# An order of its own for the first group of layer 1: four tiles' projections and turns ahead of the fifth tile's

## The chip, the cores and the metric

The kernel runs on one core of one Trainium2 chip. The metric is the device time of one execution in microseconds. A core has a matrix engine (TensorE, PE in the profile), a vector engine (VectorE, DVE), a scalar engine (ScalarE, ACT), GpSimd (POOL) and a queue engine (SyncE, SP) that here issues DMAs. "PEld" is the loading of weights into the matrix engine.

## The reference, cut to what matters

Two trunk layers work on 512 latent tokens and 256 context tokens of width 1024. Layer 0 is differential attention, layer 1 is 2-D neighbourhood attention; each is followed by a squared-ReLU MLP. The change lies in layer 1, whose mixer is, for 16 heads of 64:

```python
q_l = heads_q(h_lat, w_q, NA_HEADS, q_gain)        # project, then RMS norm per head
k_l, v_l = heads_kv(h_lat, w_kv, NA_HEADS, k_gain)
k_c, v_c = heads_kv(h_ctx, w_kv, NA_HEADS, k_gain)
...
s_all = concat(q @ k_band + bias (a window of the grid), q @ k_c)
o = softmax(s_all) @ (v_band, v_c)
y_l = o @ w_o
```

The result of layer 1 is asked for latent tokens alone, so the two context tiles need keys and values and no queries.

## The kernel before

**Tiles and products.** The 768 tokens are six tiles of 128: tiles 0 and 1 are context, tiles 2 to 5 latent. "The fifth tile" is tile 4. Each product is made of three matmuls on split operands: an operand is kept as a rounded part and a remainder, and `PASSES` runs three of the four combinations. Splitting a weight tile is `wsplit`: a copy on ACT (L146) and a subtraction (L152), which in layer 1 DVE makes.

**Layer 1's attention** works in eight groups of two heads (`group1`). A group's steps, each called by a word of an order:

- `Q0a` to `Q5b` (`project`): the projection of one token tile, in two halves of 12 matmuls (L414), 256 columns wide for tiles 0 and 1 and 384 for the others, into a bank "PA" of which there are three (`PS_ATTN1`, A=3). Behind the second half comes `qk_normed`: ACT copies the queries and keys out of the bank (L421), squares them (L425); DVE sums (L427); POOL takes the power -0.5 (L302); DVE scales (L429). The values are split beside it, by ACT (L626) and DVE (L627, the last reader of the bank).
- `U0`, `U2`, `U4` (`turn`): the normed queries and keys of two tiles are transposed by PE into a bank PA (L640 queries, L642 keys), scaled and split by ACT and DVE (L442, L443 for queries; L450 to L454 for keys) with copies on POOL (L456). `U0` also issues the load of the group's bias on SP (L635).
- `S`, `T`, `V`: scores, transposed weights, weighing.
- `w0` to `w3`: SP loads a raw weight tile of the next group (L130, two buffers R). `c0` to `c3`: that tile is split. They are not steps of the group itself.

**Order.** `run` goes through the words of an order and calls the step of group c, c-1 (one prime) or c-2 (two). Words of groups that do not exist are skipped. The instructions of PE, SP and POOL keep this order (`PINNED`), and so do the splits among each other (`pinned=True`); the other instructions of ACT and DVE are placed by a scheduler when the kernel is built, so an order does not fix their sequence. On the chip each engine goes through the sequence that it was given.

For the first group (c = 0) no earlier group exists, so what is left of `CYCLE1` is

```
w0 w1 Q0a Q1a c0 w2 Q0b Q1b Q2a Q2b Q3a Q4a c1 w3 Q3b U0 Q4b c2 U2 Q5a Q5b c3
```

and the next group's order begins with `Q0a U4' Q1a`, so that the turn of tiles 4 and 5 of the first group comes behind `Q0a` of the second. The first group's own weights are loaded and split before the end of layer 0's MLP, into buffers H; the later groups' lie in buffers W. The first projections run between the last matmuls of that MLP (L986) and the transposes of its result (L334), whose modulated parts for layer 1 are made by ACT (L337) and DVE (L339, L340) two tiles at a time, tiles 4 and 5 last.

Of the kernel before, what the change touches and what calls it, by code (L numbers as in the profile page):

```python
# [26 lines left out]
GROUPS1 = 8  # L27
# [18 lines left out]
X6 P4b V5' P5a P5b O4' O5'"""  # L46
CYCLE1 = """w0 w1 Q0a T3'' U4' Q1a c0 w2 V2'' V3'' Q0b S0' Q1b Q2a S1' Q2b Q3a T0' S2' Q4a c1 w3 T1' Q3b S3' V0' U0
Q4b c2 U2 Q5a T2' Q5b c3 V1'"""
LAST1 = """Q0a T3'' U4' Q1a c0 x0 x1 V2'' V3'' Q0b S0' Q1b X0 x2 Q2a S1' Q2b X1 Q3a T0' S2' Q4a T1' Q3b X2 S3' V0'
U0 Q4b U2 Q5a T2' Q5b V1'"""  # L50
END1 = """x3 x4 T3'' c1 U4' V2'' V3'' S0' X3 x5 P2a S1' c2 X4 P3a T0' S2' X5 T1' P4a B0 S3' V0' V1' P2b T2' x6 P3b
# [976 lines left out]
class Mods:  # L1028
# [5 lines left out]
    def load(self, early=False):  # L1034
        if self.todo:
            self.ready.append(self.b.mod_load(*self.todo.pop(0), early))
# [16 lines left out]
def run(order, c, steps, load, split, **others):  # L1053


    for word in order.split():
        kind, num, h = word[0], word[1:].rstrip("'"), c - word.count("'")
        if kind == "w":
            load(h + 1, int(num))
        elif kind == "c":  # L1060
            split(h + 1, int(num))
        elif kind in others:
            others[kind](num)
        elif h in steps:
            steps[h](kind, 2 * int(num[0]) + (num[1:] == "b") if kind == "Q" else int(num))


def hybrid_block(tc, a, out):
    nc = tc.nc
    with ExitStack() as ctx, ExitStack() as st:  # L1070
# [9 lines left out]
        with b.psum_phase("ps0", **PS_HEAD0):  # L1080
# [7 lines left out]
            heads = {0: b.head0(0, accs=accs)}  # L1088
        w = {1: b.load_qkv(a["wqa"], 1, "WB")}
        with b.psum_phase("psA", **PS_ATTN0):  # L1090
            proj, raws = {}, {}

            def load(h, k):
                if h < HEADS0:
                    raws[h, k] = b.wraw(a["wqa"][h, k], 768)

            def split(h, k):
                if h < HEADS0:
                    w.setdefault(h, []).append(b.wsplit(raws.pop((h, k)), 768, tag=("WA", "WB")[h % 2], pinned=True))
                elif k < 3:  # L1100
                    proj["weights"](k)

            with tc.manual_schedule(engines=PINNED):
                heads[1] = b.head0(1, w[1], hT)
                for c in range(2, HEADS0):
                    if c == HEADS0 - 1:
# [7 lines left out]
                own = {"P": lambda n: proj["step"](2 * int(n[0]) + (n[1] == "b")), "B": lambda _: proj["begin"](),  # L1114
                       "x": lambda n: proj["fetch"](int(n)),
                       "X": lambda n: proj["split"](int(n), (nc.gpsimd, nc.vector)[int(n) % 3 == 2])}
# [3 lines left out]
        with b.psum_phase("psB", **PS_MLP0):  # L1120
# [11 lines left out]
            w1 = []  # L1132
# [23 lines left out]
        with b.psum_phase("psC", **PS_ATTN1):  # L1156
            heads, done, proj, w, raws = {}, [], {}, {0: w1}, {}

            def load(g, k):
                if g < GROUPS1:  # L1160
                    raws[g, k] = b.wraw(a["wqb"][g, k], 768)

            def split(g, k):
                if g < GROUPS1:
                    w.setdefault(g, []).append(b.wsplit(raws.pop((g, k)), 768, eng=nc.vector, tag="W1", pinned=True))
                else:
                    proj["weights"](k)

            with tc.manual_schedule(engines=PINNED):
                own = {"P": lambda n: proj["step"](2 * int(n[0]) + (n[1] == "b")), "B": lambda _: proj["begin"](),  # L1170
                       "x": lambda n: proj["fetch"](int(n)),
                       "X": lambda n: proj["split"](int(n), nc.gpsimd)}
                for c in range(GROUPS1):
                    if c == GROUPS1 - 1:
                        b.close("W1")
                        b.open("right", W=1, ST=2)
                        proj.update(b.project(1, a["wob"], b.oT1, 2, lambda i: b.x2[i - 2], 'HQ', 'QH', 'S1', done))
                    heads[c] = b.group1(c, w.setdefault(c, []), hT1, split=proj.get("split_last"))
                    run(CYCLE1 if c < GROUPS1 - 1 else LAST1, c, heads, load, split, **own)
                b.close("W1")  # L1180
                b.open("left", W=3)
                run(END1, GROUPS1, heads, load, split, **own)
            proj["end"]()
            xh1, hT3 = done
# [82 lines left out]
```

## Time and profile before

| what | us |
|---|---|
| median of 3 runs (1872.67 to 1874.06) | 1873.72 |
| the profiled execution, its own time | 1877.93 |
| its span | 1876.1 |
| PE busy in the span | 1750.8 |
| DVE busy | 1265.9 |
| POOL busy | 1025.6 |
| ACT busy | 948.6 |

The rows of the trace come from the profiled execution and are counted from the start of its span; about 1.8 us of its time lie outside the span. Layer 1's first group of attention lies at about 1105 to 1154 us.

### The profile page before, as it was taken

To read this page: it belongs to the slowest core of one execution; us is meant where nothing else is said; L and a number is where in the kernel's file an instruction comes from. 1 tells how busy PE (TensorE), PEld (TensorE's weight loads), DVE (VectorE), ACT (ScalarE), POOL (GpSimd) and SP (SyncE) were. 2 spreads that over 40 slices of the span, in tenths; PEclk is the share of its full clock that TensorE was granted. 3 is DMA by queue.
4 is the path that set the end of the run, shared out by engine and by line. 5 is a ranking of instruction groups with operands and counts; after the bars stand their busy time and mean duration, and the time that the engine had idled before them with its cause. 6 is when DMAs were issued, how large, how long until landed. Compare 5 with 4: busy or idle time off the path is not lost.

```text
span 1876.1 us, 27723 instructions
## 1 busy us (share of the span) xinstructions
PE 1750.8 (93%) x10046; PEld 1530.5 (82%) x10046; DVE 1265.9 (67%) x2333; ACT 948.6 (51%) x2002; POOL 1025.6 (55%) x962
## 2 busy tenths in 40 slices
PE   6989999996999999999999998999998989999988
PEld 5868888984789888888887987988997777887766
DVE  4587777786665465465466776777777567777685
ACT  4476777765344333333333345777776354544432
POOL 3655666653335565555555633343345557788774
PEclk9999999997999999999999998999998989999989
DMA  8122222224536656646642321121212434334432
GB/s 332 43 85 79 88 87 70 68 84 149 175 115 167 180 163 169 186 163 173 181 162 86 118 96 59 61 87 66 65 61 90 141 103 133 124 124 149 142 116 77
DMA packets 88554, 225.97 MB, mean 120 GB/s; under 512 B 9248, under 2 KB 24544, under 8 KB 82272
## 3 DMA queue, kind: packets, MB, share of 16 engines
q1 hardware_dynamic: 78928, 211.19, 35.0%
q10 hardware_dynamic: 9488, 13.00, 1.9%
q8 instruction: 79, 1.29, 0.3%
q14 instruction: 59, 0.48, 0.1%
HBM read 205.91 MB, written 18.25 MB: 119 GB/s over the span
## 4 chain that ended last, share of the span: by engine, by line
PE 62%; DVE 11%; ACT 8%; POOL 8%; issue 6%; DMA 5%; ACTq 0%; POOLq 0%; DVEq 0%
PE PD L850 18%; PE PA L414 14%; POOL W L152 6%; PE PB L910 5%; PE PA L910 5%; PE PA L758 4%; DMA R<-in_w_dram 3%; PE PA L986 2%; PE PB L558 2%; PE PA L263 2%; ACT W L146 2%; PE PS L523 2%; PE PQ L404 1%; PE PS L662 1%; PE PB L707 1%
## 5 line engine op out<-in xcount | busy, mean ns | idle before, releaser
L152 POOL TENSOR_TENSOR W<-R,W 128x512 fp32r<-128x512 f32 x270 | 406.6, 1533 | 164.9 <-ACT W L146 162.8
L850 PE MATMUL PD<-Q,W 128*128 128x384 f32 (+2 forms) x1992 | 390.5, 346 | 12.5 <-DVE Q L340 5.9
L850 PEld LDWEIGHTS PD<-Q,W 128*128 128x128 f32 x1992 | 345.9, 189 | 43.8 <-issue 7.8
L146 ACT ACTIVATE W<-R 128x1024 fp32r<-128x1024 f32 (+1 forms) x165 | 168.2, 1023 | 201.0 <-PE PD L850 35.3
L152 POOL TENSOR_TENSOR W<-N,W 128x512 fp32r<-128x512 f32 x98 | 137.8, 1427 | 141.9 <-ACT W L146 141.6
L910 PE MATMUL PB<-W,H 128*128 128x512 f32 x738 | 191.9, 396 | 6.4 <-DVE Q L918 4.4
L910 PE MATMUL PA<-W,H 128*128 128x512 f32 x732 | 191.1, 397 | 5.1 <-DVE H L918 4.0
L414 PE MATMUL PA<-W,Q 128*128 128x384 f32 (+1 forms) x1008 | 176.3, 327 | 1.1 <-ACT H L452 1.1
L910 PEld LDWEIGHTS PB<-W,H 128*128 128x128 f32 x738 | 139.1, 190 | 38.9 <-DVE Q L918 5.3
L910 PEld LDWEIGHTS PA<-W,H 128*128 128x128 f32 x732 | 137.7, 190 | 38.1 <-DVE H L918 5.7
L302 POOL TENSOR_TENSOR SQ<-SQ,half 128x4 f32<-128x4 f32 (+1 forms) x96 | 94.0, 980 | 126.7 <-DVE SQ L427 125.6
L414 PEld LDWEIGHTS PA<-W,Q 128*128 128x128 f32 x1008 | 160.3, 193 | 1.3 <-ACT H L452 1.3
L146 ACT ACTIVATE W<-N 128x1024 fp32r<-128x1024 f32 x49 | 51.9, 1058 | 149.1 <-PE PA L910 66.4
L414 PE MATMUL PA<-WB,H 128*128 128x384 f32 x576 | 108.5, 340 | 0.8 <-DVE Q L475 0.8
L758 PE MATMUL PA<-W,H 128*128 128x512 f32 x384 | 96.9, 402 | 6.4 <-ACT H L749 4.4
L414 PEld LDWEIGHTS PA<-WB,H 128*128 128x128 f32 x576 | 98.7, 188 | 1.8 <-DVE Q L475 1.1
L850 PE MATMUL PD<-H,W 128*128 128x512 f32 (+1 forms) x408 | 94.7, 382 | 0.0
L868 DVE SCALAR_TENSOR_TENSOR H<-N,H 128x512 fp32r<-128x512 f32 (+1 forms) x57 | 66.3, 1167 | 39.8 <-ACT H L867 39.5
L758 PEld LDWEIGHTS PA<-W,H 128*128 128x128 f32 x384 | 71.6, 192 | 24.1 <-ACT H L749 4.8
L529 ACT ACTIVATE E<-PS,SA 128x768 f32<-128x768 f32 (+1 forms) x96 | 73.0, 760 | 35.3 <-DVE SA L528 32.0
L528 DVE TENSOR_REDUCE SA<-PS 128x1 f32<-128x768 f32 (+1 forms) x96 | 74.5, 776 | 21.0 <-ACT E L529 11.5
L850 PEld LDWEIGHTS PD<-H,W 128*128 128x128 f32 x408 | 75.0, 192 | 14.9
(258 smaller groups left out, 3563.4 us busy)
## 6 DMA issues: line engine op xcount, KB each, us to landing
R<-in_w_dram SPq DMA_DIRECT2D x121, 512.0 KB
M<-in_wmod_dram SPq DMA_DIRECT2D x48, 1024.0 KB
N<-in_w_dram SPq DMA_DIRECT2D x49, 512.0 KB
R<-in_wqa_dram SPq DMA_DIRECT2D x32, 384.0 KB
R<-in_wqb_dram SPq DMA_DIRECT2D x32, 384.0 KB
Y<-in_rpb_dram SPq DMA_DIRECT2D x48, 128.0 KB
bias<-Y SPq DMA_DIRECT2D x48, 128.0 KB
X<-bias SPq DMA_DIRECT2D x8, 768.0 KB
```

What stands on the lines that cost most here:

```text
L146: high = nc.scalar.activation(w[:, 0, :n], raw, AF.Copy)
L152: low = (eng or nc.gpsimd).tensor_sub(w[:, 1, o:e], raw[:, o:e], w[:, 0, o:e].bitcast(F32))
L263: nc.tensor.matmul(ps[32 * q:32 * q + 32, 0:256], self.silu[:, kt, :], raws[kt], start=kt < 4, stop=kt >= 4)
L302: nc.gpsimd.tensor_tensor(r, ss, self.half[:, :n], op=ALU.pow)
L414: nc.tensor.matmul(acc[:, :n], hT[kt][:, x, P * i:P * i + P], w[kt // 2][:, y, o:o + n], start=(kt == 0 and p == 0), stop=(kt == KT - 1 an ...
L523: nc.tensor.matmul(s[:, c0:c1], q[:, m, P * i:P * i + P], k[:, m, c0:c1], start=p == 0, stop=p == 1)
L528: nc.vector.tensor_reduce(mx, s, op=ALU.max, axis=AX, negate=True)
L529: nc.scalar.activation(e[:, m, :nk], s, AF.Exp, bias=mx[:, 0:1], accum_out=sm[:, m:m + 1])
L758: nc.tensor.matmul(ps, oHL[h][:, x, c:c + P], w[h // 2][:, y, 512 * (h % 2):512 * (h % 2) + 512], start=(first and h == hs[0] and p == 0), ...
L850: nc.tensor.matmul(ps[:, at:at + b1 - b0], w[kt // 4][:, x, o:o + P], hT[kt][:, y, b0:b1], start=(kt == 0 and p == 0), stop=(kt == KT - 1 ...
L868: nc.vector.scalar_tensor_tensor(u[:, 1], src, 1.0, u[:, 0].bitcast(F32), op0=ALU.mult, op1=ALU.subtract)
L910: nc.tensor.matmul(ps, u[:, x, f, P * i:P * i + P], w[:, y, 512 * f:512 * f + 512], start=(f == 0 and p == 0), stop=(f == 1 and p == 2))
```

## The change

The first group gets an order of its own, `START1`. It names each word once, so that nothing is added to or taken from the work; words without a step for c = 0 are not written.

```diff
+START1 = """w0 w1 Q0a Q1a c0 Q0b Q1b w2 Q2a Q2b Q3a U0 Q3b c1 w3 U2 Q4a Q4b c2 Q5a Q5b c3"""
 LAST1 = ...
@@
                     heads[c] = b.group1(c, w.setdefault(c, []), hT1, split=proj.get("split_last"))
-                    run(CYCLE1 if c < GROUPS1 - 1 else LAST1, c, heads, load, split, **own)
+                    run(START1 if c == 0 else CYCLE1 if c < GROUPS1 - 1 else LAST1, c, heads, load, split, **own)
```

Against what was left of `CYCLE1`: up to `Q3a` the matmuls stand as before. `U0` moves ahead of `Q3b`; `U2` moves ahead of `Q4a` and stands right behind `Q3b` (with `c1 w3` between, which are not PE's); `Q4a` moves behind `U2`, so that both halves of tiles 4 and 5 run in one piece. `c1` and `w3` move behind `Q3b`, `w2` behind `Q1b`, and with it the load of the bias in `U0` stands ahead of `w3` on SP.

## Rows read from the trace of the kernel before

**Rows 1.** The page: busy time of each engine.
```profile
PE 1750.8 (93%) x10046; PEld 1530.5 (82%) x10046; DVE 1265.9 (67%) x2333; ACT 948.6 (51%) x2002; POOL 1025.6 (55%) x962
```

**Rows 2.** Timeline of PE: start, duration, line, count [idle before, releaser].
```profile
1118.60 3.96 PE L414 MATMUL PA<-H,Q 128*128 128x256 f32 x26
...
1122.43 1.31 PE L414 MATMUL PA<-H,Q 128*128 128x384 f32 x6
...
1123.60 1.48 PE L414 MATMUL PA<-H,Q 128*128 128x384 f32 x7
...
1127.48 0.66 PE L334 MATMUL PB<-ident,N 128*128 128x128 f32 x4 [0.26 <-ACT Y L337]
1131.78 9.13 PE L414 MATMUL PA<-H,Q 128*128 128x384 f32 x36 [3.64 <-DVE H L627]
1140.75 0.38 PE L642 MATMUL PA<-ident,Y 128*128 128x128 f32 x2
1140.88 2.36 PE L414 MATMUL PA<-H,Q 128*128 128x384 f32 x12
1143.08 0.27 PE L640 MATMUL PA<-ident,Y 128*128 128x128 f32 x1
...
1144.13 0.33 PE L640 MATMUL PA<-ident,Y 128*128 128x128 f32 x1 [0.68 <-DVE Y L429]
...
1144.46 4.49 PE L414 MATMUL PA<-H,Q 128*128 128x384 f32 x24
1148.79 1.59 PE L414 MATMUL PA<-W,Q 128*128 128x256 f32 x12
...
1153.80 0.33 PE L640 MATMUL PA<-ident,Y 128*128 128x128 f32 x1 [3.20 <-DVE Y L429]
...
1153.99 4.61 PE L414 MATMUL PA<-W,Q 128*128 128x256 f32 x24
```

**Rows 3.** Timeline of ACT, same columns.
```profile
1125.50 3.76 ACT L337 ACTIVATE Y<-PB,mB,mA 128x256 f32<-128x256 f32 x8 [4.45 <-PE PB L334]
...
1129.87 0.28 ACT L421 ACTIVATE Y<-PA 128x128 f32<-128x128 f32 x1
...
1130.92 0.90 ACT L146 ACTIVATE W<-R 128x768 fp32r<-128x768 f32 x1
...
1149.21 0.39 ACT L421 ACTIVATE Y<-PA 128x256 f32<-128x256 f32 x1
...
1149.79 0.85 ACT L146 ACTIVATE W<-R 128x768 fp32r<-128x768 f32 x1
```

**Rows 4.** Timeline of DVE, same columns.
```profile
1131.44 0.68 DVE L627 TENSOR_TENSOR H<-PA,H 128x128 fp32r<-128x128 f32 x3
...
1134.68 0.29 DVE L429 SCALAR_TENSOR_TENSOR Y<-Y,SQ 128x128 f32<-128x128 f32 x1
...
1150.67 0.96 DVE L152 TENSOR_TENSOR W<-R,W 128x768 fp32r<-128x768 f32 x1 [0.58 <-ACT W L146]
```

**Rows 5.** PE in slices of 2 us: width, busy (count), granted clock, DMA share, GB/s.
```profile
84.00:86.00 2.00, 1.53 (x10) 1.00 0.00 0
...
1130.00:1132.00 2.00, 0.22 (x1) 0.64 0.00 0
...
1136.00:1138.00 2.00, 2.00 (x9) 0.66 0.86 352
...
1154.00:1156.00 2.00, 2.00 (x13) 0.61 0.08 22
```

**Rows 6.** Timeline of PE, a wait in layer 0.
```profile
84.47 0.66 PE L505 MATMUL PC<-ident,Y 128*128 128x128 f32 x4 [3.35 <-ACT Q L452]
```

**Rows 7.** Timeline of SP.
```profile
1131.55 1.79 SPq L130 DMA_DIRECT2D R<-in_wqb_dram  x2
1133.39 0.43 SPq L635 DMA_DIRECT2D X<-bias  x1
```

## The prediction

> **What bounds the kernel now.** I read the page first: PE is busy 93% of the span, DVE 67%, the others less [rows 1]. So the time is PE's, and a reordering that leaves the work alone can only win or lose PE's idle time and its clock. Then I read PE's timeline through the first group of layer 1 and looked for every idle stretch with its releaser [rows 2]. There are three. PE has nothing to run from 1128.14 (the four transposes from 1127.48 last 0.66) to 1131.78, 3.64 us, until DVE's L627 releases a bank PA. It waits 0.68 us inside `U2` (1144.13) and 3.20 us inside `U4'` of the next group (1153.80), both times for the normed tile (L429). Then I read ACT and DVE over the same stretch to see what makes those releases late [rows 3, 4], and the granted clock in slices of 2 us [rows 5]. The clock matters: after the first wait it is at its lower level (0.5 of 2.4 GHz, 1.2 GHz), and after the third again.
>
> The 36 matmuls from 1131.78 are `Q3a`, `Q4a`, `Q3b`; they take 8.97 us up to the next row, while 24 of the same width take 4.33 us from 1144.46 to 1148.79, 0.180 each [rows 2]. At full clock the 36 would take 6.5 us. The slice 1130 to 1132 has a mean clock of 0.64, that of 1136 to 1138 has 0.66 [rows 5]: of the latter two microseconds x ran at half, 0.5x + (2 - x) = 1.32, so x = 1.36 and the clock rose at 1137.36. From 1131.78 that is 5.58 us at half; the rest, 3.39 us, holds 18.8 matmuls at 0.180, so the first 17.2 took 0.32 each. These are the two prices I use.
>
> **What stays.** Up to `Q3a` PE's sequence is the old one, so the wait of 3.64 us stays as long as ACT and DVE keep their sequence. Tiles 0 to 2 have 72 matmuls, and the last 13 of them are the 6 and 7 from 1122.43 and 1123.60, so by 1122.6 tiles 0 and 1 (48) are complete [rows 2]. Yet ACT reads out the first of them at 1129.87, behind its eight modulations of tiles 4 and 5, for which it had idled 4.45 us [rows 3]; DVE's L627, three in 0.68 us from 1131.44, then frees the banks of tiles 0, 1 and 2 [rows 4]. The second and third of these banks are what `U0` and `U2` will take, so no wait for a bank is added. No instruction is added or removed; PE's matmuls, transposes and the DMAs are the same number.
>
> **The moved steps, in the new sequence.**
> 1. `Q3a` from 1131.78: 12 at 0.32 is 3.84, to 1135.62.
> 2. `U0`: its inputs are ready, the last one, tile 1, is scaled by 1134.97 [rows 4]. It costs PE 0.13 (1140.75 to 1140.88 [rows 2]), some more at the low clock, I take 0.18: 1135.80. Its key splits now run on ACT and DVE beneath `Q3b` and are covered by it.
> 3. `Q3b`: 4.9 matmuls until 1137.36, the other 7.1 at 0.180: to 1138.64. It ends 2.1 us earlier than before (1140.75), because `Q4a` no longer stands ahead of it.
> 4. `U2` now stands right behind. Tile 2 is ready, but tile 3 has to go through copy, square, sum, power and scale first, and PE has nothing else: behind `U2` in its queue stand `Q4a` to `Q5b`, all of whose operands are there. Before, `Q4b` covered this (2.20 us from 1140.88 to 1143.08) and only 0.68 us of idle time were left [rows 2]. The price is the length of the chain, and the trace has it twice: from the end of `Q3b` to the release of `U2`, 1140.75 to 1144.13, is 3.38 us; from the end of `Q5b` to the release of `U4'`, 1148.79 to 1153.80, is 5.01 us [rows 2]. The difference is a weight split: behind `Q5b` comes `c3`, and ACT runs its L146 (0.85 us from 1149.79) ahead of the square, DVE its L152 (0.96 from 1150.67) ahead of the sum [rows 3, 4]. In the new order `c1` stands right behind `Q3b` as `c3` stands behind `Q5b`; before, it was run at 1130.92, in the shade of the first wait [rows 3]. Bounds: 3.38 and 5.01. I take 4.7, near the long end, because the instance with a split right behind it is the alike one, less the 0.3 by which ACT came late to its copy there (1149.21 against 1148.95, the end of the matmuls). So `U2` is released at 1143.34; before, at 1144.13.
> 5. `Q4a` starts 0.33 behind that release, as 1144.46 behind 1144.13: 1143.67. Then 48 matmuls at 0.180, 8.66 us: the next group's `Q0a` starts at 1152.33, against 1148.79 before. That is **+3.5 us** (+2.2 with the short chain, +3.9 with the long one).
> 6. The clock. PE idles some 4.5 us in step 4. The wait of 3.20 us before 1153.80 was followed by the lower clock (slice 1154 to 1156 at 0.61 [rows 5]), and its 24 matmuls took 4.61 us where 12 at full clock took 1.59 [rows 2]: 1.4 us lost. A wait of 3.35 us in layer 0 [rows 6] shows 1.00 in its slice [rows 5], so a fall is not certain. Bounds 0 and 2.5 (what 36 matmuls lost after the first wait, 8.97 - 6.5); I take **+1.5**, 3.4 us at half (10.6 matmuls, each 0.14 dearer), which is nearer to the third wait's loss.
> 7. Behind `Q5b` nothing changes in kind: `c3`, tile 5's chain, `Q0a` and `U4'` follow as before, and I take the third wait and its clock unchanged. From there on the order is `CYCLE1` and the shift is handed on, since PE stays the bound.
> 8. DMAs: `w2` was issued when `c0` freed its buffer (1131.55) and the bias behind `w3` (1133.39) [rows 7]. Now the bias goes first and `w3` waits for `c1`, some 10 us later, about 1142; it is needed by `c3` at about 1152, and the bias by the scores of the next group. Cover is enough, cost nothing; without it, `c3` would be late and with it the next group's second halves. POOL's copies of `U0` now stand ahead of tile 3's power; they fall at 1137 to 1139, before it (about 1140.9): nothing.
>
> Step 6 has a rule beside it. The Trainium skill, "TensorE: Matmul & The Clock Gate", Part 1, says that the throttled state is the default and that activity releases it, so that a starved engine goes back to the low rate. By that rule the new wait costs clock, and the time is 1878.7; by the row of layer 0 alone it would be 1877.2. The trace agrees with the rule at two of the three waits above 3 us named here.
>
> **Sum.** 3.5 + 1.5 = 5.0 us, put on the profiled execution 1877.93 + 5.0 = 1882.9. That execution is 4.2 above the median of the runs, so for the runs I say 1873.7 + 5.0 = **1878.7** (+0.27%). About 0.2%, 3.75 us, is what a measurement here can tell from no change.
>
> **Rivals.**
> *Half of it (0.28).* The wait comes, but either `c1`'s split falls outside tile 3's chain (its tile lies ready long before, so the scheduler may run it beneath `Q3b`, where ACT and DVE have room), or the clock holds. Then +2.2 to +3.9: 1875.9 to 1877.6. For it: layer 0's wait without a fall; ACT's sequence is not the order's. Against: `c3` and its place right behind L421.
> *Given back at `U4'` (0.20).* `U2`'s splits are further ahead of tile 5's chain, and `c3` may drop out of it if `w3` lands later in the scheduler's plan. A chain of 3.38 in place of 5.01 gives 1.6 us, with the clock's 1.4 saved as well 3.0. With the forecast that nets +0.5 to +3.4: 1874.2 to 1877.1. Against: `c3` keeps its place behind `Q5b`.
> *Faster (0.12).* With another order behind it, the scheduler puts the read-out of tiles 0 and 1 into ACT's 4.45 us of idle time ahead of the modulations. Then the first wait goes, `Q3a` starts at 1128.1 at full clock; `Q3a`, `U0`, `Q3b` end at 1132.6, `U2` is released at 1137.3, and `Q0a` starts at 1146.3, 2.5 earlier than before, or 1.0 if the clock falls at `U2`; with the short chain 3.8. Time 1869.9 to 1872.7. It decides if ACT's first L421 of this group comes ahead of the eight L337. For it: the banks are full and ACT idle. Against: the sequence up to there has the same steps in the same order.
>
> **Numbers.** The forecast has 0.40, its own range 1877.2 to 1880.0. Slower by over 0.2%: most of the forecast (0.37), a third of half of it (0.08), and a remainder (0.02): 0.47. Faster: 0.10 of the last rival and 0.01: 0.11. Same: 0.42. The range reaches from 1872.5, which leaves out the stronger half of the faster case, to 1881.0, a long chain and a longer stretch at half clock: 3.9 + 2.5 = 6.4, and 1 us more.
>
> **What would show it.** Right: PE's wait inside `U2` grows from 0.68 us to 3 to 5 us; L146 of `c1` stands between L421 and L425 of tile 3; a slice at half clock behind `U2`; `Q0a` of the second group some 3 to 5 us later behind the first 36-matmul row's start; groups two to eight alike. Wrong: no wait of 3.64 us ahead of `Q3a`, or a wait at `U4'` that is far below 3.2.

## The result, and the profile after

The change costs time: 1879.25 us median of 13 runs against 1875.58 of the kernel before, measured beside it, 13 runs too. The measured ratio is 1.0023, 95% interval 1.0014 to 1.0033; the two medians alone give 1.0020. That is the way that was forecast, inside the range, and most of the size: 3.7 us by the medians and 4.3 by the ratio, where +5.0 us (0.27%) was forecast. The profiled execution has a span of 1881.6 us.

PE's timeline of the changed kernel, the stretch of [rows 2] (all lines are one further down than before):

```profile
1128.09 0.66 PE L335 MATMUL PB<-ident,N 128*128 128x128 f32 x4 [0.26 <-ACT Y L338]
1132.38 3.69 PE L415 MATMUL PA<-H,Q 128*128 128x384 f32 x12 [3.64 <-DVE H L628]
1135.92 0.38 PE L643 MATMUL PA<-ident,Y 128*128 128x128 f32 x2
...
1138.24 0.27 PE L641 MATMUL PA<-ident,Y 128*128 128x128 f32 x1
...
1143.35 0.45 PE L641 MATMUL PA<-ident,Y 128*128 128x128 f32 x1 [4.72 <-DVE Y L430]
...
1143.66 11.08 PE L415 MATMUL PA<-H,Q 128*128 128x384 f32 x48
1154.58 1.59 PE L415 MATMUL PA<-W,Q 128*128 128x256 f32 x12
...
1159.24 0.45 PE L641 MATMUL PA<-ident,Y 128*128 128x128 f32 x1 [2.86 <-DVE Y L430]
...
1159.55 4.47 PE L415 MATMUL PA<-W,Q 128*128 128x256 f32 x24
1163.86 1.12 PE L663 MATMUL PS<-H,H 128*128 128x256 f32 x8
...
1182.52 0.41 PE L643 MATMUL PA<-ident,Y 128*128 128x128 f32 x2
```

The reader sees the same first wait, 3.64 us, then `Q3a`, `U0`, `Q3b` in the new order, and then the wait inside `U2`: 4.72 us in place of the 0.68 of [rows 2]. Its chain, from the end of `Q3b` (1138.24) to the release (1143.35), is 5.11 us. From the start of `Q3a` to the second group's `Q0a` it is 22.20 us, before 17.01: +5.19.

For the comparisons below I use one stretch: from the last four transposes of the MLP's result to `U0` of the second group. Here it is 1128.09 to 1182.52, 54.43 us. Before it is 1127.48 to 1177.09 (timeline of PE, the row below), 49.61:

```profile
1177.09 0.41 PE L642 MATMUL PA<-ident,Y 128*128 128x128 f32 x2
```

So +4.82 us. The rest of the 5.5 us between the two spans lies elsewhere: 0.61 had been added by the transposes of 1128.09 (a second execution of the changed kernel, experiment 5, has them at 1127.67), and 0.1 comes after the stretch. The kernel before has one profiled execution, and the stretch is not the same in every execution of one kernel: 54.43 and 53.58 us in the two of the changed kernel.

What fills tile 3's chain is seen on ACT and DVE of the changed kernel:

```profile
1138.44 0.38 ACT L422 ACTIVATE Y<-PA 128x256 f32<-128x256 f32 x1 [0.48 <-PE PA L415]
1138.85 0.38 ACT L453 ACTIVATE H<-PA 64x256 fp32r<-64x256 f32 x1
...
1139.43 0.83 ACT L147 ACTIVATE W<-R 128x768 fp32r<-128x768 f32 x1
1140.16 0.41 ACT L426 ACTIVATE sq<-Y 128x256 f32<-128x256 f32 x1
```

```profile
1140.30 0.96 DVE L153 TENSOR_TENSOR W<-R,W 128x768 fp32r<-128x768 f32 x1 [0.44 <-ACT W L147]
1141.17 0.42 DVE L428 TENSOR_REDUCE SQ<-sq 128x4 f32<-128x260 f32 x1
```

`c1`'s copy (L147) stands between the copy and the square of tile 3, its subtraction (L153) ahead of the sum, as `c3`'s do behind `Q5b` [rows 3, 4]. A key split of `U0` (L453) stands behind tile 3's copy too. The granted clock, in slices of 2 us as in [rows 5]:

```profile
1130.00:1132.00 2.00, 0.00 (x0) 0.97 0.00 0
...
1134.00:1136.00 2.00, 2.00 (x10) 0.67 1.02 421
...
1142.00:1144.00 2.00, 0.65 (x3) 0.53 0.69 197
...
1148.00:1150.00 2.00, 2.00 (x10) 0.76 0.00 0
...
1160.00:1162.00 2.00, 2.00 (x11) 0.50 0.04 8
```

After the first wait it is low from 1131.88 to 1135.32, half as long as before (1130.56 to 1137.36 by the same reckoning from [rows 5]); behind `U2` it is low from 1142.1 to 1149.0, and the 48 matmuls take 10.92 us (8.66 at the price of [rows 2]). It falls a third time behind `U4'`, as before the change: 24 matmuls take 4.31 us up to the next row, 4.45 before.

### The profile page after: what moved, and what is told of

Its sections match the earlier page's. It is cut to its first block, busy times and chain, and to the rows that moved or that the text cites. A ratio compares the mean times of both kernels' runs of the same rounds, so it can differ in the third digit from the quotient of the medians.

```text
span 1881.6 us, 27726 instructions
## 1 busy us (share of the span) xinstructions
PE 1748.6 (93%) x10046; PEld 1528.6 (81%) x10046; DVE 1267.7 (67%) x2333; ACT 947.2 (50%) x2002; POOL 1024.6 (54%) x962
## 4 chain that ended last, share of the span: by engine, by line
PE 63%; DVE 11%; ACT 8%; POOL 8%; issue 6%; DMA 5%; ACTq 0%; POOLq 0%; DVEq 0%
PE PD L851 17%; PE PA L415 15%; POOL W L153 6%; PE PB L911 5%; PE PA L911 5%; PE PA L759 4%; DMA R<-in_w_dram 3%; PE PA L987 2%; PE PB L559 2%; PE PA L264 2%; ACT W L147 2%; PE PS L524 2%; PE PQ L405 1%; PE PS L663 1%; PE PB L708 1%
## 5 line engine op out<-in xcount | busy, mean ns | idle before, releaser
L153 POOL TENSOR_TENSOR W<-R,W 128x512 fp32r<-128x512 f32 x270 | 403.8, 1524 | 163.6 <-ACT W L147 163.0
L147 ACT ACTIVATE W<-R 128x1024 fp32r<-128x1024 f32 (+1 forms) x165 | 168.0, 1021 | 198.3 <-DMA R<-in_w_dram 34.6
L153 POOL TENSOR_TENSOR W<-N,W 128x512 fp32r<-128x512 f32 x98 | 139.0, 1439 | 144.2 <-ACT W L147 140.0
L147 ACT ACTIVATE W<-N 128x1024 fp32r<-128x1024 f32 x49 | 51.8, 1058 | 149.5 <-PE PA L911 66.5
```

The costliest lines, as they stand in the source:

```text
L147: high = nc.scalar.activation(w[:, 0, :n], raw, AF.Copy)
L153: low = (eng or nc.gpsimd).tensor_sub(w[:, 1, o:e], raw[:, o:e], w[:, 0, o:e].bitcast(F32))
```

## The experiments

Theory A: the loss is PE's uncovered wait for tile 3 in `U2`, which `c1`'s split lengthens, and the lower clock behind it. Rivals: the later `c1` and `w3` and the new order of DMAs (B); or that PE's idle time is not what sets the pace here, since ACT and DVE's splits would hold the second group up anyway (C).

**1. `U2` alone put back.**

```diff
-... Q3a U0 Q3b c1 w3 U2 Q4a Q4b c2 Q5a Q5b c3
+... Q3a U0 Q3b c1 w3 Q4a Q4b c2 U2 Q5a Q5b c3
```

> The new order with U2 alone put back behind Q4b; U0 early, c1 and w3 behind Q3b, the bias ahead of w3, Q4a behind Q3b all stay. Theory A (the loss is PE's uncovered wait for tile 3 in U2 and the clock behind it): 24 matmuls, 4.3 us, cover a chain of 4.8 us, so the wait in U2 falls from 4.72 us to under 0.5, the clock does not fall there, and the second group's Q0a starts about 15.5 us behind the start of Q3a (17.0 before, 22.2 after the change): the time is 5 to 6.5 us below the changed kernel, that is 0 to 1.5 us below the kernel before, the same by any clock of runs. Theory B (the later c1 and w3 and the other order of DMAs cost the time): nothing comes back, 22 us and 1.0023.

PE's timeline:

```profile
1136.70 6.77 PE L415 MATMUL PA<-H,Q 128*128 128x384 f32 x36
...
1144.10 0.33 PE L641 MATMUL PA<-ident,Y 128*128 128x128 f32 x1 [0.41 <-DVE Y L430]
...
1148.60 1.59 PE L415 MATMUL PA<-W,Q 128*128 128x256 f32 x12
...
1153.96 0.34 PE L641 MATMUL PA<-ident,Y 128*128 128x128 f32 x1 [3.55 <-DVE Y L430]
```

The wait in `U2` is 0.41 us, the clock does not fall there, `Q0a` comes 16.2 us behind `Q3a` (at 1132.41), the stretch is 49.14 us. Ratio 0.9991 (0.9982 to 1.0001). All of the loss comes back although `c1`, `w3`, the bias and the early `U0` stay in their new order: B is out. What `U2`'s later place costs is seen at `U4'`, where 3.55 us are waited and not 2.86.

**2. `c1`'s split taken out of tile 3's chain,** run twice.

```diff
-... Q3a U0 Q3b c1 w3 U2 ...
+... Q3a c1 w3 U0 Q3b U2 ...
```

> The new order with c1 and w3 ahead of U0, so that ACT and DVE run c1's split at once, before tile 3's chain. Theory A: the wait in U2 shrinks by the split's share of the chain, from 4.72 to about 3.4 us; the second group's Q0a starts 19.2 (clock stays) to 20.9 us (clock falls) behind Q3a; 1.3 to 3 us below the changed kernel, 1.5 to 4 above the kernel before. Theory B (c1 and w3 late): all of it comes back, 17 us and ratio 1.000.

> The kernel with c1 and w3 ahead of U0 once more. Its trace had a shorter wait in U2 (3.42 us), but new waits ahead of S0' (0.56 and 0.77 us) and a stretch of 54.88 us against 49.61 before, while its runs gave 1.0008 (0.9996 to 1.0021). If the trace is right in general: the same waits, a stretch of 53 to 55 us and a ratio of 1.0018 to 1.003. If the runs are: a stretch near 51 and 1.0008 again.

PE's timeline and ACT's of the second of the two:

```profile
1139.39 0.27 PE L641 MATMUL PA<-ident,Y 128*128 128x128 f32 x1
...
1143.20 0.30 PE L641 MATMUL PA<-ident,Y 128*128 128x128 f32 x1 [3.43 <-DVE Y L430]
...
1162.70 0.87 PE L663 MATMUL PS<-H,H 128*128 128x256 f32 x6
1164.13 0.39 PE L663 MATMUL PS<-H,H 128*128 128x256 f32 x1 [0.56 <-ACT H L453]
1165.29 0.39 PE L663 MATMUL PS<-H,H 128*128 128x256 f32 x1 [0.77 <-DVE H L455]
```

```profile
1162.90 0.28 ACT L422 ACTIVATE Y<-PA 128x128 f32<-128x128 f32 x1 [1.85 <-PE PA L415]
...
1163.70 0.38 ACT L453 ACTIVATE H<-PA 64x256 fp32r<-64x256 f32 x1
```

The wait shrinks from 4.72 to 3.42 and 3.43 us: 1.3 us is the split's price in the chain. But the stretch does not shrink, 54.88 and 55.06 us. In this build ACT has the second group's first copy (L422) ahead of a split of `U4'` (L453); the copy waits 1.85 us for PE, and the split, which was ready, stands behind it. `S0'` then waits 0.56 and 0.77 us, and from its first matmul to the next row it takes 2.81 us, 1.9 more than in the changed kernel (0.96). Ratios 1.0008 (0.9996 to 1.0021) and 1.0017 (1.0005 to 1.0029): lower than the changed kernel's, but not told apart from it. So in the traces the split's share was real and was given back two steps later by the scheduler's other sequence; whether a part of it stayed, the runs leave open.

**3. The split doubled.** `c2` stands beside `c1` behind `Q3b`.

```diff
-... Q3b c1 w3 U2 Q4a Q4b c2 Q5a Q5b c3
+... Q3b c1 c2 w3 U2 Q4a Q4b Q5a Q5b c3
```

> The changed kernel with c2 beside c1 behind Q3b, so that two weight splits stand in tile 3's chain. If a split in the chain costs what was read from the trace (about 1.3 us), the wait in U2 goes from 4.72 to about 6.0, and the second group's Q0a from 22.2 to 23.5 us behind Q3a at equal clock: ratio 1.002 to 1.004. If the chain is set by POOL's power and the fixed latencies, the wait stays at 4.7.

PE's timeline, ACT's and DVE's:

```profile
1145.91 0.44 PE L641 MATMUL PA<-ident,Y 128*128 128x128 f32 x1 [5.59 <-DVE Y L430]
...
1146.22 9.85 PE L415 MATMUL PA<-H,Q 128*128 128x384 f32 x48
```

```profile
1141.12 1.56 ACT L147 ACTIVATE W<-R 128x768 fp32r<-128x768 f32 x2
```

```profile
1141.99 1.83 DVE L153 TENSOR_TENSOR W<-R,W 128x768 fp32r<-128x768 f32 x2 [0.44 <-ACT W L147]
```

The wait grows by 0.87 us, to 5.59, and not by the expected 1.3: the second copy on ACT runs while DVE subtracts the first, so only one of the two engines' times counts again. `Q0a` comes 23.1 us behind `Q3a` (at 1132.80). Ratio 1.0030 (1.0018 to 1.0042), as expected, but not told apart from the changed kernel's 1.0023.

**4. The wait filled,** to measure the clock's share. 22 matmuls are added between `U2`'s transposes of tile 2 and of tile 3, into a bank that nobody reads.

```diff
+                if g == 0 and i0 == 2 and j == 0:
+                    fill = self.pst('B')
+                    for k in range(22):
+                        nc.tensor.matmul(fill[:, :384], hT[k % 8][:, 0, 0:P],
+                                         w[k % 8 // 2][:, 0, 384 * (k % 2):384 * (k % 2) + 384],
+                                         start=k == 0, stop=k == 21)
```

> The changed kernel with 22 matmuls added between U2's transposes of tile 2 and tile 3 (384 wide, into a bank that nobody reads), about 4 us of work in a wait of 4.72 us: extra work that the result does not use. It measures the clock's share. If the lower clock behind the wait is part of the loss: the 48 matmuls behind U2 take 8.7 us and not 10.9, and the kernel with the extra work is 2.2 us faster than the changed kernel, about 2.7 above the kernel before. If the clock's part is an accident of the one trace: no difference from the changed kernel, ratio 1.0023.

PE's timeline, and the slice behind `U2`:

```profile
1131.27 4.21 PE L415 MATMUL PA<-H,Q 128*128 128x384 f32 x12 [3.64 <-DVE H L628]
...
1138.45 4.11 PE L647 MATMUL PB<-H,Q 128*128 128x384 f32 x22
1143.43 0.30 PE L641 MATMUL PA<-ident,Y 128*128 128x128 f32 x1 [0.87 <-DVE Y L430]
...
1143.59 8.70 PE L415 MATMUL PA<-H,Q 128*128 128x384 f32 x48
1152.13 1.58 PE L415 MATMUL PA<-W,Q 128*128 128x256 f32 x12
...
1156.96 4.62 PE L415 MATMUL PA<-W,Q 128*128 128x256 f32 x24
```

```profile
1144.00:1146.00 2.00, 2.00 (x14) 1.00 0.00 2
```

With the wait filled the clock stays at 1.00 and the 48 matmuls take 8.54 us, 2.4 less. Yet the runs show no gain: 1.0027 (1.0015 to 1.0040), and the expected 2.2 us are missed. The stretch is 53.09 us, 1.3 below the changed kernel's. The fall at `U4'` does not explain why it is not 2.4, for the profiled execution above has that fall too (24 matmuls and the next row's start: 4.46 us here, 4.31 there). What differs is the first wait: behind it the clock stays low longer here, and from the start of `Q3a` to the end of `Q3b` it takes 7.05 us against 5.86. Against the second execution of the changed kernel (53.58 us, next) the stretch is 0.5 us shorter: 1.5 are won behind `U2` and 1.1 lost behind `U4'`, where that execution has no fall. So the clock's share behind `U2` is seen in the trace alone; intervals of some 0.1% (2 us) on either side do not let the runs show or exclude it.

The trace settles something else. In this execution the clock falls where it fell before the change: behind the first wait, low for 6.8 us in both, and behind `U4'` (4.46 and 4.45 us), but not in between. `Q0a` comes 20.86 us behind the start of `Q3a`, 3.85 more than before, and the stretch is 3.48 us longer. That is what the uncovered wait costs at equal clock, by one execution of either kernel.

**5. The changed kernel once more.**

> The changed kernel itself once more, beside the others on the same chip. The waits (3.64, 4.72 and 2.86 us) are set by sequences and should come back to 0.05 us. The clock behind them need not: if the lower clock behind U2 belongs to a wait of that length, the 48 matmuls take 10.2 to 10.9 us again; if it was chance, 8.7. Ratio 1.0015 to 1.0033.

PE's timeline, and further down that of the wait in layer 0 [rows 6]:

```profile
1131.97 4.21 PE L415 MATMUL PA<-H,Q 128*128 128x384 f32 x12 [3.64 <-DVE H L628]
...
1139.09 0.27 PE L641 MATMUL PA<-ident,Y 128*128 128x128 f32 x1
...
1144.19 0.30 PE L641 MATMUL PA<-ident,Y 128*128 128x128 f32 x1 [4.72 <-DVE Y L430]
...
1144.36 10.24 PE L415 MATMUL PA<-H,Q 128*128 128x384 f32 x48
1154.43 1.58 PE L415 MATMUL PA<-W,Q 128*128 128x256 f32 x12
...
1159.26 3.10 PE L415 MATMUL PA<-W,Q 128*128 128x256 f32 x24
```

```profile
85.49 0.66 PE L506 MATMUL PC<-ident,Y 128*128 128x128 f32 x4 [3.35 <-ACT Q L453]
85.90 5.98 PE L415 MATMUL PA<-WB,H 128*128 128x384 f32 x24
```

The three waits are the same to 0.01 us. The 48 matmuls take 10.07 us, so the clock fell again behind `U2`; behind `U4'` it stayed up this time, and 24 matmuls took 2.94 us. Of the 1.4 us that this wins there, 0.4 go again in `S0'`, which takes 1.35 us and not 0.96. Stretch 53.58 us, ratio 1.0021 (1.0010 to 1.0032).

**6. The first wait.** The order of before, with `c0` and `w2` behind `Q2b`.

```diff
-w0 w1 Q0a Q1a c0 w2 Q0b Q1b Q2a Q2b Q3a Q4a ...
+w0 w1 Q0a Q1a Q0b Q1b Q2a Q2b c0 w2 Q3a Q4a ...
```

> The order of before with c0 and w2 moved behind Q2b. It asks what makes the first wait of 3.64 us, which the change left alone. If it is the position of tile 0's read-out on ACT and DVE: c0's copy and subtraction (0.84 and 0.95 us) no longer stand ahead of it, the wait shrinks by 1.0 to 1.3 us to about 2.4, and the time falls by that, or by up to 3.5 us if the clock then does not fall: ratio 0.998 to 0.9995. If the modulation of tiles 4 and 5 alone sets it, the wait stays 3.6 and the time the same.

PE's timeline:

```profile
1131.45 8.14 PE L415 MATMUL PA<-H,Q 128*128 128x384 f32 x36 [2.43 <-DVE H L628]
```

It shrinks to 2.43 us, by the 1.2 that `c0`'s copy and subtraction took ahead of tile 0's read-out; the rest is the modulation's. The clock still falls, but stays low for 3.4 us and not 6.8, so that the 36 matmuls take 7.97 us and not 8.97. Of these 2.2 us little arrives: the stretch is 49.23 us, only 0.4 shorter, for `S0'` has the waits of experiment 2 (0.56 and 0.78 us) here too and takes 1.9 us more than before. Ratio 0.9989 (0.9977 to 1.0001).

**7. The third wait.** The order of before, and an order of its own for the second group, with `U4'` behind `Q1a` and `S0'` behind `Q1b`.

```diff
+SECOND1 = """w0 w1 Q0a T3'' Q1a U4' c0 w2 V2'' V3'' Q0b Q1b S0' Q2a ..."""
-CYCLE1 = ...  Q0a T3'' U4' Q1a c0 w2 V2'' V3'' Q0b S0' Q1b Q2a ...  (for c = 1)
```

> The order of before, and an order of its own for the second group: U4' behind Q1a and S0' behind Q1b, each half a projection later. The wait of 3.20 us at U4' gets 12 more matmuls (1.4 us) as cover and shrinks to 1.8. If PE's idle time is what counts: the stretch from the last four transposes of the MLP's result to U0 of the second group, 49.61 us before, is 1.4 us shorter, or up to 2.8 if the clock then stays up: ratio 0.9985 to 0.9995. If the splits on ACT and DVE behind U4' pace the second group's first scores, the same time is lost again ahead of S0', and the stretch stays at 49.6.

PE's timeline:

```profile
1155.99 0.33 PE L643 MATMUL PA<-ident,Y 128*128 128x128 f32 x1 [1.75 <-DVE Y L432]
...
1156.18 3.10 PE L417 MATMUL PA<-W,Q 128*128 128x256 f32 x24
...
1160.41 0.39 PE L665 MATMUL PS<-H,H 128*128 128x256 f32 x1 [0.42 <-ACT H L455]
1161.71 0.39 PE L665 MATMUL PS<-H,H 128*128 128x256 f32 x1 [0.91 <-DVE H L457]
```

The wait is 1.75 us and the clock stays up, which together are worth 2.9 us; 1.9 of them are lost in `S0'` (2.81 us to the next row, 0.95 before). Stretch 48.33 us, 1.3 shorter; ratio 0.9995 (0.9984 to 1.0007), nothing that the runs can tell. Here C is partly right: the splits behind `U4'` take back what is won ahead of it.

**8. All of it together,** run twice.

```diff
+START1 = """w0 w1 Q0a Q1a Q0b Q1b Q2a Q2b c0 w2 Q3a c1 w3 U0 Q3b Q4a Q4b c2 U2 Q5a Q5b c3"""
+SECOND1 = as in 7
```

> All three together: U0 early but U2 behind Q4b, c0 and w2 behind Q2b, c1 and w3 behind Q3a, and the second group's U4' behind Q1a with S0' behind Q1b. If the waits add up: first wait 2.4, none above 0.5 in U2, at most 2.2 at U4'; the stretch of 49.61 us shrinks by 2 to 4 us, ratio 0.9975 to 0.999. If the group is paced by ACT and DVE, the stretch stays above 48.5.

> The combined order once more. Its stretch was 47.64 us, 1.97 below before, which is 0.10% of the time; the runs gave 0.9987 (0.9974 to 1.0000). If the gain is real, 0.998 to 0.9995 again and a stretch of 47 to 48.5 us; if it was noise, 1.000.

PE's timeline of the second run:

```profile
1151.27 0.33 PE L643 MATMUL PA<-ident,Y 128*128 128x128 f32 x1 [0.86 <-ACT H L455]
...
1153.04 0.36 PE L643 MATMUL PA<-ident,Y 128*128 128x128 f32 x1 [1.33 <-DVE Y L432]
```

First wait 2.44, no wait in `U2`, two at `U4'` of 0.86 and 1.33; `S0'` waits as in experiment 7 (0.42 and 0.92 us). The stretch is 47.64 and 47.58 us, 2.0 shorter than before. Ratios 0.9987 (0.9974 to 1.0000) and 0.9987 (0.9975 to 0.9999): about 2.4 us, the one version here whose interval lies at or below 1, at the edge of what the runs can tell.

## Why the prediction was right

**The first wait** was to stay as it was: 3.64 us, and 3.64 in every run that kept `c0` in its place. The faster rival, which needed ACT to read out tile 0 ahead of the modulations, did not come about.

**Steps 1 to 3** gave `Q3b`'s end 6.86 us behind the start of `Q3a`. It was 5.86 in the profiled execution, where the matmuls ran at half clock for 2.9 us and not the 5.6 that the prediction took over from before, and 7.12 in the second. The length of that stretch varies from execution to execution of one order. Step 2's "covered" was not quite so: the last key split of `U0` on ACT (1138.85) came behind `Q3b`'s end, into tile 3's chain.

**Step 4, the term that decides,** was 4.7 us between the bounds 3.38 and 5.01; it measured 5.11 and 5.10 in the two executions. The choice of the end with a split was right for the reason that was given: `c1` runs where `c3` runs, and taking it out brings the chain to 3.81 us (1139.39 to 1143.20 in experiment 2). The long bound was a little short by that key split, 0.38 us ahead of tile 3's value copy.

**Step 5** holds, 0.31 and 0.17 us for 0.33. The +3.5 us that it comes to (+3.9 with the long chain) measured +3.85 at equal clock, in experiment 4.

**Step 6, the clock,** was +1.5 us with bounds 0 and 2.5. The 48 matmuls lost 2.3 and 1.4 us against 8.66. So the fall behind `U2` came both times. The Trainium skill, "TensorE: Matmul & The Clock Gate", Part 1, states that the throttled state is the default; both traces agree with it at this wait. What the prediction did not see is how much the price depends on the execution: the fall behind `U2` cost 2.3 us in one and 1.4 in the other, the third wait had its fall in the one and none in the other, and what is won behind a wait can go again in `S0'`.

**Step 7** took the third wait as unchanged. It was 2.86 in place of 3.20, because ACT had `U2`'s splits behind it and came to tile 5's copy at once: -0.3 us. Its clock was unchanged in the profiled execution and did not fall in the second.

**Step 8** holds: the order of the DMAs costs nothing, as experiment 1 shows, which keeps it and loses nothing.

**The sum:** 5.0 forecast; +4.82 and +3.97 us in the stretch of the two executions; 0.23% and 0.21% of the time, 4.3 and 3.9 us, in the runs. The mechanism is right, and the size of the wait nearly so. That the profiled execution comes within 0.2 us is luck in part: 1.0 less behind the first wait and 0.3 less at the third stand against 0.4 more in the chain and 0.8 more clock behind `U2`. With the first wait's clock as it was before, an estimate comes to 5.0 as well: the 3.48 of experiment 4, and the 1.53 by which its 48 matmuls are quicker than those of experiment 5 (10.07 - 8.54). The median of 1879.25 near the forecast's 1878.7 is in part luck too: the kernel before measured 1.9 us more in the 13 runs of the comparison than in the three on which the forecast was built.

The rival "half of it" is not what happened in the traces: the split was in the chain and the clock fell. The runs alone could not exclude its upper end. "Given back" came true by 0.3 us at the wait and, in the second execution, by the clock there; its lower end of +0.5 also left out the 1.5 of step 6, with which it would have been +2.0.

What stays open: why the clock falls at a wait in one execution and not in the next, and so what the clock's share is in the median of the runs. No run here holds it fixed.

## What to carry to other kernels

When a step is moved ahead on the engine that bounds the kernel, ask for each of its operands how long its chain is over the other engines and what matmuls are left in front of it as cover; here the change left none for a chain of 5.1 us, and with 24 matmuls (4.3 us) put back in front of it 0.41 us were waited. A piece of unrelated work that is written next to such a step (a weight split) can land in its chain: 1.3 us here, and 0.9 for a second one.

A wait that is shortened must be followed to the next join: in experiments 2, 6 and 7 some 1.9 us came up again two steps later, in `S0'`. In 2 and 6 ACT took its instructions in an order that had a copy still waiting for PE (1.85 and 1.68 us) ahead of a split that was ready.

## What the runs showed of the hardware that was not expected

At waits of 2.43 us (experiment 6) and 3.64 us alike the clock went to 1.2 GHz, and in experiment 8 it did so at `U4'`, after two waits of 0.86 and 1.33 us with only two transposes between them (24 matmuls in 4.42 us in the run above). After 3.35 us in layer 0 [rows 6] and after 2.86 us behind `U4'` in the second execution it stayed at 2.4. The same waits went the other way as well: the 2.86 us of the profiled execution were followed by a fall (0.50 in the slice 1160 to 1162), and so were the 3.35 us of layer 0 in the second, whose 24 matmuls took 5.98 us, against 4.44 in the kernel before. So the length of the wait alone does not decide.

How long the clock stayed low also differed: of the nine traces with the first wait of 3.64 us it was 3.4 us in one, the changed kernel's profiled execution, and 6.8 in the others. After the 2.43 and 2.44 us of experiments 6 and 8 it was 3.4 us in all three traces.
